# A hybrid attention and gated-recurrence layer: the recurrence's output gate as seven-product blocks, its queries computed ahead, its VectorE steps and root rewritten

## The chip, the cores and the metric

The kernel runs on one core of one Trainium2 chip. A core has a matrix engine (TensorE, PE in the profile, with PEld for its weight loads), three elementwise engines (VectorE or DVE, ScalarE or ACT, GpSimd or POOL) and SyncE (SP), which here issues DMA transfers. Each engine takes its own instructions in their order, and semaphores make one wait for another. The metric is the device time of one execution in microseconds.

## The reference

One layer on x (1024 tokens by 1024 channels, float32). After an RMS norm a single projection gives everything: queries, keys and values of 24 attention heads, a gate path for attention, and for the recurrence q, two forget gates, an input i and an output gate g, and two merge gates.

```python
z = einsum('bsd,dc->bsc', h, w_in)
qkv_a, g_a, q_b, zf_fwd, zf_bwd, i_b, g_b, zgate_a, zgate_b = split(z, split_points)
...
f = lb + (1.0 - lb) * sigmoid(z_f)                  # per direction
o = gla_chunk_scan(q_b, 1.0 - f, i_b, log(f))       # S_t = diag(f_t) S_{t-1} + k_t v_t^T, o_t = S_t^T q_t
...
o_b = rms_norm(o_fwd + o_bwd, hg_norm_w) * silu(g_b)
merged = sigmoid(zgate_a) * y_a + sigmoid(zgate_b) * y_b
out = x + merged @ w_out
```

Attention normalises its queries and keys per head (`rms_norm` again), in three groups of dilated windows. The recurrence has 8 heads of 128 channels and runs forwards and backwards.

## The kernel before, in words

**Arithmetic.** Big products are made in three passes: a float32 operand is split into a rounded high part and the rest (`whi` and `wlo` for weights, `hh` and `hl` for activations), and high by high, high by low and low by high are added up in PSUM. Each pass is a matmul of 128x128 weights by 512 columns. A weight page (128x512) comes by DMA, ACT rounds it (`whi<-raw` or `whi<-qraw`), and POOL, DVE or an adding DMA makes the rest (`wlo`).

**What sets the order.** The builder writes the program with a planner at its side. Each call is booked on a clock per engine (`note`, line 139), work that isn't a big product is queued as tasks with a priority and a condition, and after every few matmuls `tick` (line 253) and `burst` (line 269) put those into the program that the clocks call ready. The result is one fixed order of instructions on each engine. On the chip an engine that is late against these clocks delays all that stands behind it.

**The stages, in order.**

1. Values of the three attention groups as plain products (`gp` in the rows).
2. Blocks of seven products (`run_quads`, line 433): a pair of 512-channel halves by a pair of 512-token halves in 7 products of 12 matmuls in place of 8, as in Strassen's scheme. The products 11, T2, T3 and T4 go one after another into one PSUM bank (`qA`), T1 and 22 into a second (`qE`), 21 into a third (`qC`). After 11, T1 and T2 ACT copies the bank out (`spare<-qA`, `stage<-qA`, `spare<-qE`) before the next product adds to it; T4 is copied at the block's end. There are 20 blocks in the order twelve times `qk` (queries and keys) and eight others: groups of `qk qk sg`, six times, then `ga ga`. A `qk` result goes through the norm of its heads: ACT squares it and rounds the square (`ny<-spare`, `nhi<-ny`), PE sums over a head (`nss`), and `guess` (line 1072) makes the inverse root on ACT with Ln, Exp and Square; `newton` on DVE corrects it. `sg` (merge gates) is only stored. `ga` (attention's gate) goes through Sigmoid on ACT (`ga_sig`, line 1120). Before the stage one table of ACT's functions that has Ln and Exp is set (`blocks_start`, line 1011).
3. Attention and its merge, with the projections for the recurrence's input i and gate g between them (`evac_early`, line 1514): for each of four pairs of heads 8 groups of 24 matmuls, whose 512 columns are 256 of i and 256 of g, stored to `igD`.
4. The recurrence, head by head. Six groups of 24 matmuls a head: four for the two forget gates by two halves (`evac_f`, with Sigmoid in the copy) and two for q (`evac_q`). Between them, as small matmuls and tasks: `logs` (ACT), `sums` (DVE: k, scan `Bc`, differences), `exps_b` (ACT), `k_mul` (POOL), `q_mul` and `k_state` (DVE), transposes `kT`, states `U` and `S`, cross products `X` and `Y`, outputs `oB`, `norm_out` (DVE: root and product with the gate), transpose `onT`. The gate's Sigmoid is `gate_sig` on ACT. Merge gates (eight groups of 24) end the stage.
5. The last projections as seven products again (`sA`, `sE`), and the residual.

A tile's first letters name it in the profile; all work is booked through one helper, so all rows bear line 56 (57 in the changed kernel).

Of the kernel before, what the change touches and what calls it, by code (L numbers as in the profile page):

```python
# [27 lines left out]
TAIL, LATE = 4, 4  # L28
QRAW, SPARE = 6, 7
# [84 lines left out]
class Plan:  # L114
# [5 lines left out]
    def __init__(self, nc):  # L120
        self.nc = nc
        self.t = dict(pe=0.0, act=0.0, dve=0.0, pool=0.0, sp=0.0)
        self.port = 0.0
        self.wire = 0.0
        self.w, self.r = Book(), Book()
        self.wide = True
# [12 lines left out]
    def note(self, key, op, args, kw):  # L139
        if op == "preload_act_table_set":  # L140
            self.t["act"] += 1.3
            return
# [14 lines left out]
        for x in outs:  # L157
            start = max(start, self.w.last(x, key, self.HOP), self.r.last(x, key, self.HOP))
        if op == "dma_start":
# [6 lines left out]
        else:  # L166
# [45 lines left out]
class Builder:  # L212
# [128 lines left out]
    def feed(self):  # L341

        if self.raw_next < len(self.wpages):
            t = self.rawr.get()
            self.p.sp.dma_start(t, self.wpages[self.raw_next])
# [227 lines left out]
def hybrid_block(ctx, tc, a, out):  # L573
# [41 lines left out]
    ig_pages = lambda pr: some(100 + 20 * pr, 8)  # L615
# [5 lines left out]
    for k in range(6):  # L621
        blocks += qk[2 * k:2 * k + 2] + sg[k:k + 1]
    blocks += [("ga", 0), ("ga", 2)]

    def block_pages(kind, *at):
        if kind == "sg":
            return (*gate_pages(*at), *gate_pages(at[0], at[1] + 1))
        if kind == "ga":
            return tuple(some(72 + 2 * at[0], 4))
        g, hv, e = at  # L630
# [6 lines left out]
    for pr in range(4):  # L637
        items += ig_pages(pr)
    for j in range(TAIL, LATE):
        items += gate_pages(1, j)  # L640
    for h in range(8):
        items += zf_pages(h) + q_pages(h)
# [152 lines left out]
    igD = dr.tile([4, 8, 128, 512], F32, name="igD")  # L795
# [315 lines left out]
    def put_ga(j):  # L1111
        def f(half, col, z, mine):
# [4 lines left out]
            b.task("act", [z], lambda: ga_sig(j + col, half, z, ring), 3, blk["y"].soon)  # L1117
        return f

    def ga_sig(j, half, z, ring):  # L1120
# [8 lines left out]
        def out():  # L1129
            s_.dma_start(gaD[j, half], z)  # L1130
# [8 lines left out]
    b.run_quads(A, [{"qk": put_qk, "sg": put_sg, "ga": put_ga}[x[0]](*x[1:]) for x in blocks],  # L1139
# [374 lines left out]
    def evac_early(pr, i):  # L1514
        def f(ps):
# [3 lines left out]
            store(igD[pr, i], t)  # L1519
        return f  # L1520

    for pr in range(4):
# [8 lines left out]
        pos += 8  # L1531
    merge_maybe(True)
# [22 lines left out]
    nomlb = hp.tile([128, 2, 8], F32, name="nomlb")  # L1555
    a_.activation(lb, mx, AF.Sigmoid)
    v_.tensor_scalar(omlb, lb, -1.0, 1.0, op0=OP.mult, op1=OP.add)
    v_.tensor_scalar(nomlb, omlb, -1.0, None, op0=OP.mult)
# [13 lines left out]
    ig_ring = b.ring(hp, "ig", 8, [128, 512])  # L1572
    sk_ring = b.ring(hp, "sk", 5, [128, 512])
    qq_ring = b.ring(hp, "q", 3, [128, 512])
    lf_ring = b.ring(hp, "lf", 4, [128, 512])
    q2_ring = b.ring(hp, "q2", 4, [128, 4, 64])
    km_ring = b.ring(hp, "km", 4, [128, 512])
    qr_ring = b.ring(hp, "qr", 4, [128, 512])
# [7 lines left out]
    GI = set()  # L1586
    SK, QQ = {}, {}
    H = {}

    def load_ig(pr, i):  # L1590
        t = ig_ring.get()
        s_.dma_start(t, igD[pr, i])
        IG[pr, i] = t

    def gate_sig(pr, i):

        t = on_ring.get()
        for k in range(2):
            a_.activation(t[:, 256 * k:256 * k + 256], IG[pr, i + k][:, 256:512], AF.Sigmoid)
        b.task("dve", [t], lambda: gate_mul(pr, i, t), 5)  # L1600

    def gate_mul(pr, i, t):
        for k in range(2):
            g = IG[pr, i + k][:, 256:512]
            v_.tensor_tensor(g, g, t[:, 256 * k:256 * k + 256], op=OP.mult)
        on_ring.done(t)
        GI.add((pr, i))
# [25 lines left out]
    def start_head(h):  # L1633
        st = dict(mm=[None, None], G=[None, None], QR={}, Q2={}, KM={}, S={}, s=0, qm=0, km=0)
# [3 lines left out]
        b.task("act", [SK[h, d, u] for d, u in ORDER], lambda: logs(h), 4, lambda: lf_ring.soon(4))  # L1638

    def logs(h):  # L1640
        a_.preload_act_table_set("natural_log_exp_and_others")
        for d, u in ORDER:
            lf = lf_ring.get()
# [3 lines left out]
    def sums(h, d, u, lf):  # L1647
        st = H[h]
        sk = SK[h, d, u]
        v_.tensor_scalar(sk, sk, nomlb[:, d, h:h + 1], omlb[:, d, h:h + 1], op0=OP.mult, op1=OP.add)  # L1650
# [6 lines left out]
        for k, e in enumerate((MID1[d], MID2[d], LAST[d])):  # L1657
            g_.tensor_copy(st["mm"][d][:, k, 4 * u:4 * u + 4], B4[:, :, e])
# [7 lines left out]
        b.task("act", [D1, Q2], lambda: exps_b(h, d, u, D1, Q2), 4, lambda: km_ring.soon() and qr_ring.soon())  # L1666

    def exps_b(h, d, u, D1, Q2):
# [3 lines left out]
        a_.activation(c4(KM)[:, :, fst], c4(D1)[:, :, fst], AF.Exp, scale=-1.0)  # L1672
        a_.activation(c4(KM)[:, :, sec], Q2, AF.Exp, scale=-1.0)
        QR = qr_ring.get()
        a_.activation(QR, D1, AF.Exp)
        a_.activation(Q2, Q2, AF.Exp)
        lf_ring.done(D1)
        st["QR"][d, u], st["KM"][d, u] = QR, KM
        b.task("pool", [KM], lambda: k_mul(h, d, u), 3)
        if h % 2 == 0 and len(st["QR"]) == 4:  # L1680
            for i in range(0, 8, 2):
                b.task("act", [], lambda i=i: gate_sig(h // 2, i), 4, lambda i=i: (h // 2, i + 1) in IG and on_ring.soon())
# [4 lines left out]
    def decay(h, d):  # L1687
# [5 lines left out]
        v_.tensor_tensor(t[:, cur], mm[:, 2, cur], mm[:, 0, nxt], op=OP.add)  # L1693
        v_.tensor_tensor(G[:, cur, d], t[:, cur], mm[:, 0, cur], op=OP.subtract)
        v_.tensor_tensor(G[:, cur, 1 - d], t[:, cur], mm[:, 1, cur], op=OP.subtract)
# [38 lines left out]

    def k_state(h, d, u):
# [4 lines left out]
        ks = SK.pop((h, d, u))  # L1740
# [582 lines left out]
```

## Time and profile before

| what | value |
|---|---|
| median of 3 runs (lowest, highest) | 1514.19 us (1513.56, 1517.37) |
| the profiled execution, its span | 1514.28 us, 1512.5 us |
| instructions | 23147, of which 8013 matmuls |
| busy: PE, DVE, ACT, POOL | 1472.8, 1004.8, 873.7, 411.2 us |
| stage 2, seven-product blocks | from 148.2 us to about 563 |
| stage 4, recurrence | from about 869 us to 1305 |

The span runs from the first to the last instruction. In the profile's rows an engine's busy time comes with its count of instructions; a mean is that of one instruction; what stands behind the bar is the time that the engine idled just before instructions of that group, and whom it waited for. One fp32 matmul that isn't split (128x128 by 128) shows as two.

### The profile page before, as it was taken

Reading aid. Unit: us, or ns where it says so; the run is one execution under the profiler, and the core shown is the slowest. Engines: PE = TensorE matmul, PEld = TensorE weight load, DVE = VectorE, ACT = ScalarE, POOL = GpSimd, SP = SyncE. Lnnn points to the kernel's source line nnn. Section 1 sums busy time; section 2 is a strip of 40 time slices with the busy share of each in tenths; the row PEclk is TensorE's granted clock in tenths of the full one; section 3 lists DMA queues with packets and bytes.
Section 4 is the critical chain, followed back from the end, with each engine's and each line's share of the span. In section 5 each row is a group of like instructions: output and inputs, shape, how many; then the busy total and the mean of one; then the engine's idle time right before and its main releaser. Section 6 shows DMA issues by size and latency. Waiting matters only on the chain.

```text
span 1512.5 us, 23147 instructions
## 1 busy us (share of the span) xinstructions
PE 1472.8 (97%) x8013; PEld 1211.2 (80%) x8013; DVE 1004.8 (66%) x2061; ACT 873.7 (58%) x1788; POOL 411.2 (27%) x436
## 2 busy tenths in 40 slices
PE   8999999999999999999999998999999999999998
PEld 6788878778788887888877787888878888887787
DVE  6791677678878854545423636988688887259873
ACT  5542667476676755676742266575567664447451
POOL 0032334344443340020023342333244322000011
PEclk9999999999999999999999999999999999999999
DMA  6454465755744347566265673353434524775554
GB/s 201 134 201 161 155 200 120 193 110 135 175 112 119 99 131 262 173 215 190 84 169 181 190 207 68 70 140 78 132 65 90 135 65 101 209 237 167 168 154 132
DMA packets 181067, 224.08 MB, mean 148 GB/s; under 512 B 45084, under 2 KB 101428, under 8 KB 180437
## 3 DMA queue, kind: packets, MB, share of 16 engines
q1 hardware_dynamic: 158980, 195.67, 40.5%
q0 software_dynamic: 14544, 26.48, 11.3%
q10 hardware_dynamic: 7424, 0.45, 0.3%
q8 instruction: 63, 1.03, 0.3%
q14 instruction: 56, 0.45, 0.1%
HBM read 166.61 MB, written 77.43 MB: 161 GB/s over the span
## 4 chain that ended last, share of the span: by engine, by line
PE 59%; ACT 3%; issue 3%; DVE 3%; DMA 2%; POOL 1%; SPq 0%; POOLq 0%; ACTq 0%; DVEq 0%
PE gp L56 25%; PE sA L56 6%; PE qA L56 5%; PE sE L56 4%; PE qE L56 3%; PE o L56 3%; PE oB L56 3%; PE pT L56 2%; PE sc L56 2%; PE U L56 1%; PE qC L56 1%; PE X L56 1%; ACT L56 1%; DMA raw<-in_w_in_dram 1%; DVE Bc L56 1%
## 5 line engine op out<-in xcount | busy, mean ns | idle before, releaser
L56 POOL TENSOR_TENSOR wlo<-qraw,whi 128x512 fp32r<-128x512 f32 x100 | 148.2, 1487 | 259.4 <-ACT whi L56 230.5
L56 PE MATMUL gp<-whi,hh 128*128 128x512 f32 x344 | 139.2, 405 | 3.2 <-ACT stage L56 1.8
L56 PE MATMUL gp<-hh,whi 128*128 128x512 f32 x336 | 137.6, 409 | 0.0
L56 PE MATMUL gp<-whi,hl 128*128 128x512 f32 x344 | 134.8, 392 | 1.4 <-DVE hl L56 1.3
L56 PE MATMUL gp<-wlo,hh 128*128 128x512 f32 x344 | 134.5, 391 | 1.4 <-POOL wlo L56 1.4
L56 PE MATMUL gp<-hh,wlo 128*128 128x512 f32 x336 | 131.9, 392 | 0.0
L56 PE MATMUL gp<-hl,whi 128*128 128x512 f32 x336 | 131.4, 391 | 0.0
L56 ACT ACTIVATE whi<-qraw 128x512 fp32r<-128x512 f32 x140 | 86.9, 626 | 72.2 <-DVE qraw L56 48.6
L56 POOL TENSOR_TENSOR wlo<-raw,whi 128x512 fp32r<-128x512 f32 x46 | 64.6, 1417 | 234.9 <-ACT whi L56 232.4
L56 ACT ACTIVATE whi<-raw 128x512 fp32r<-128x512 f32 x120 | 74.9, 626 | 85.5 <-PE gp L56 66.1
L56 DVE CUSTOM_DVE_ANT_0 as<-sc,abias 128x192 f32<-128x192 f32 (+2 forms) x192 | 56.0, 348 | 91.8 <-PE sc L56 71.4
L56 ACT ACTIVATE stage<-gp 128x512 f32<-128x512 f32 x60 | 35.6, 598 | 108.2 <-PE gp L56 71.9
L56 DVE TENSOR_TENSOR qraw<-qraw,qraw 128x512 f32<-128x512 f32 x80 | 66.5, 832 | 42.7 <-DMA qraw<-in_w_in_dram 21.5
L56 POOL DMA_DIRECT2D wlo<-in_w_in_dram x49 | 43.4, 885 | 162.3 <-ACT wlo L56 144.0
L56 ACT ACTIVATE as<-as,neg 128x192 f32<-128x192 f32 (+2 forms) x192 | 83.5, 439 | 6.1 <-DVE neg L56 6.1
L56 PEld LDWEIGHTS gp<-whi,hh 128*128 128x128 f32 x344 | 64.6, 188 | 23.3 <-issue 4.8
L56 PEld LDWEIGHTS gp<-whi,hl 128*128 128x128 f32 x344 | 64.6, 188 | 16.6 <-DVE hl L56 3.0
L56 PEld LDWEIGHTS gp<-wlo,hh 128*128 128x128 f32 x344 | 64.7, 188 | 14.7 <-POOL wlo L56 2.7
L56 PEld LDWEIGHTS gp<-hh,wlo 128*128 128x128 f32 x336 | 63.3, 189 | 14.0
L56 PEld LDWEIGHTS gp<-hl,whi 128*128 128x128 f32 x336 | 63.7, 190 | 11.2
L56 PEld LDWEIGHTS gp<-hh,whi 128*128 128x128 f32 x336 | 63.6, 189 | 11.0
L56 ACT ACTIVATE ny<-ny 128x512 f32<-128x512 f32 x96 | 60.7, 633 | 11.4 <-DVE ny L56 5.5
(295 smaller groups left out, 4179.0 us busy)
## 6 DMA issues: line engine op xcount, KB each, us to landing
raw<-in_w_in_dram SPq DMA_DIRECT2D x112, 256.0 KB
qraw<-in_w_in_dram SPq DMA_DIRECT2D x80, 256.0 KB
wlo<-in_w_in_dram POOLq DMA_DIRECT2D x49, 256.0 KB, 3.9
qkD<-ny SPq DMA_DIRECT2D x48, 256.0 KB
igD<-stage SPq DMA_DIRECT2D x32, 256.0 KB
ig<-igD SPq DMA_DIRECT2D x32, 256.0 KB
sg<-sgD SPq DMA_DIRECT2D x32, 256.0 KB
eraw<-wsD SPq DMA_DIRECT2D x32, 256.0 KB
```

The costliest lines, as they stand in the source:

```text
L56: got = f(*args, **kw)
```

## The change

It has six parts.

- **The output gate g.** It leaves the plain products of stage 3. Four new blocks `gb` of seven products stand in stage 2, one behind each of the first four groups (`qk qk sg gb`); their results go through `ga_sig` (Sigmoid on ACT, product on DVE, in place) to `gbD`, one row per channel. Stage 3 has then two sets of 8 groups for i alone (`ibD`).
- **The queries q.** Their 16 groups move from stage 4 to stage 3, behind those of i, and are stored to `qD`; stage 4 loads them again, and loads the gate.
- **VectorE's steps.** k is no longer made by a DVE instruction of its own: `exps_b` adds log(1-lb) to its exponents on ACT, and `k_mul` makes (sigmoid - 1) times that on DVE, where it stood on POOL before; the minus sign is undone by the corrected root (its factor -0.5 is left out with 1/256 in `onw`). The forget gate's copy is a plain copy now, and its Sigmoid a second ACT instruction in `logs`, four in a row.
- **The root.** `norm_out`'s eleven small DVE instructions become Ln, Exp, Square on ACT and two on DVE, then four scaled copies on ACT; the gate is multiplied in behind the transpose, by one DVE instruction that also empties the bank.
- **The rings.** i takes 8 tiles of half the width, the gate 2, loaded q 2, forget gates 7 for 5; the logs, their differences and exponentials share 8 tiles.
- **The planner** books a change of ACT's function table (`self.table`), and DVE's wait for its own results.

On ACT in stage 2, inside a pair of `qk` blocks: two guesses (Ln, Exp, Square: the first reads `nss`) between two copies of a bank. Before:

```order
L56 ACTIVATE spare_2235<-qA_2103 128x512
L56 ACTIVATE whi_2244<-qraw_1956 128x512
L56 ACTIVATE ny_2253<-nss_2210,eps 128x512
L56 ACTIVATE ny_2253<-ny_2253 128x512
L56 ACTIVATE ny_2254<-ny_2253 128x512
L56 ACTIVATE whi_2265<-qraw_2141 128x512
L56 ACTIVATE ny_2272<-nss_2237,eps 128x512
L56 ACTIVATE ny_2272<-ny_2272 128x512
L56 ACTIVATE ny_2273<-ny_2272 128x512
L56 ACTIVATE whi_2290<-qraw_2133 128x512
L56 ACTIVATE stage_2316<-qA_2297 128x512
```

And in the changed kernel, in the pair behind the first `gb` block:

```order
L57 ACT_TABLE_LOAD
L57 ACTIVATE ny_2503<-nss_2452,eps 128x512
L57 ACT_TABLE_LOAD
L57 ACTIVATE ny_2503<-ny_2503 128x512
L57 ACTIVATE ny_2504<-ny_2503 128x512
L57 ACTIVATE whi_2519<-qraw_2313 128x512
L57 ACT_TABLE_LOAD
L57 ACTIVATE ny_2527<-nss_2481,eps 128x512
L57 ACT_TABLE_LOAD
L57 ACTIVATE ny_2527<-ny_2527 128x512
L57 ACTIVATE ny_2528<-ny_2527 128x512
L57 ACTIVATE spare_2542<-qA_2272 128x512
```

A load of a function table stands ahead of each Ln and each Exp now. So it is with 40 of the 48 guesses; the eight ahead of the first `gb` block have none.

On ACT in stage 4, around the first head (`km`, `lf`, `qr`, `q` belong to the forget gates, `on` to the output gate, `kT` is a transposed key). Before:

```order
L56 ACT_TABLE_LOAD
L56 ACTIVATE on_8794<-ig_8471 128x256
L56 ACTIVATE on_8794<-ig_8473 128x256
L56 ACTIVATE on_8805<-ig_8475 128x256
L56 ACTIVATE on_8805<-ig_8477 128x256
L56 ACTIVATE whi_8816<-raw_8597 128x512
L56 ACTIVATE wlo_8817<-whi_8816 128x512
L56 ACT_TABLE_LOAD
L56 ACTIVATE G_8789<-G_8789 128x14
L56 ACTIVATE kT_8827<-kT_8822 128x512
L56 ACT_TABLE_LOAD
L56 ACTIVATE sk_8845<-gp_8797 128x512
```

After, for the second head:

```order
L57 ACTIVATE kT_9467<-kT_9462 128x512
L57 ACTIVATE kT_9473<-kT_9469 128x384
L57 ACTIVATE sk_9475<-gp_9403 128x512
L57 ACT_TABLE_LOAD
L57 ACTIVATE sk_9281<-sk_9281 128x512
L57 ACTIVATE sk_9341<-sk_9341 128x512
L57 ACTIVATE sk_9475<-sk_9475 128x512
L57 ACTIVATE sk_9401<-sk_9401 128x512
L57 ACT_TABLE_LOAD
L57 ACTIVATE qr_9493<-sk_9281,lbv,omlb 128x512
L57 ACTIVATE qr_9495<-sk_9341,lbv,omlb 128x512
L57 ACTIVATE kT_9535<-kT_9530 128x512
```

Here the loads are fewer, two a head, and stand together; no key's copy stands between them.

On DVE in stage 4, first head: k (`sk`), scan (`Bc`), differences, and in the changed kernel the key product `km`. Before:

```order
L56 TENSOR_SCALAR sk_8605<-sk_8605,nomlb,omlb 128x512
L56 SCALAR_TENSOR_TENSOR Bc_8697<-rst_8437,lf_8618 128x512
L56 TENSOR_TENSOR lf_8618<-Bc_8697 128x512
L56 TENSOR_TENSOR q_2_8703<-Bc_8697 128x256
L56 TENSOR_TENSOR Gt_8740<-mm_8607 128x7
L56 TENSOR_TENSOR G_8739<-Gt_8740,mm_8607 128x7 x2
```

After:

```order
L57 SCALAR_TENSOR_TENSOR Bc_9323<-rst_9074,qr_9249 128x512
L57 TENSOR_TENSOR qr_9249<-Bc_9323 128x512
L57 TENSOR_TENSOR q_2_9328<-Bc_9323 128x256
L57 SCALAR_TENSOR_TENSOR km_9330<-sk_9130,km_9330 128x512
L57 SCALAR_TENSOR_TENSOR km_9347<-sk_9164,km_9347 128x512
L57 TENSOR_TENSOR Gt_9371<-mm_9234 128x7
L57 TENSOR_TENSOR G_9370<-Gt_9371,mm_9234 128x7 x2
```

One row is gone, and POOL's product has come in. The diff, cut to what is spoken of:

```diff
@@ note (planner)
+        if key == "dve":
+            for x in ins:
+                start = max(start, self.w.last(x) + 0.05)
...
+                need = {AF.Sigmoid: ("sig",), AF.Ln: ("ln",), AF.Exp: ("exp", "ln")}.get(args[2])
+                if need and self.table not in need:
+                    self.table = need[0]
+                    pace += 1.28
@@ pages and blocks
-    ig_pages = lambda pr: some(100 + 20 * pr, 8)
+    ib_pages = lambda k: [_dram(wi, (100 + 40 * k + d) * 65536, [[512, 128], [20 * 65536, 2], [1, 256]]) for d in range(8)]
...
-        blocks += qk[2 * k:2 * k + 2] + sg[k:k + 1]
+        blocks += qk[2 * k:2 * k + 2] + sg[k:k + 1] + ([("gb", k)] if k < 4 else [])
@@ put_ga
+    def put_gb(pr):
+        return put_ga(2 * pr, gbD)
@@ stage 3
-    for pr in range(4):
+    for pr in range(2):
...
+    for h in range(EARLY):
+        for u in range(2):
+            b.run_unit([T_group(pos, u, evac_qe(h, u), u == 1)])
+            merge_maybe()
+        pos += 2
@@ stage 4
-            a_.activation(t, ps, AF.Sigmoid)
+            a_.activation(t, ps, AF.Copy)
...
     def logs(h):
+        for d, u in ORDER:
+            a_.activation(SK[h, d, u], SK[h, d, u], AF.Sigmoid)
         a_.preload_act_table_set("natural_log_exp_and_others")
...
-        v_.tensor_scalar(sk, sk, nomlb[:, d, h:h + 1], omlb[:, d, h:h + 1], op0=OP.mult, op1=OP.add)
...
-        a_.activation(c4(KM)[:, :, fst], c4(D1)[:, :, fst], AF.Exp, scale=-1.0)
+        a_.activation(c4(KM)[:, :, fst], c4(D1)[:, :, fst], AF.Exp, scale=-1.0, bias=lomlb[:, d, h:h + 1])
...
-        g_.tensor_tensor(KM, KM, SK[h, d, u], op=OP.mult)
+        v_.scalar_tensor_tensor(KM, SK[h, d, u], -1.0, KM, op0=OP.add, op1=OP.mult)
...
-        r = rsqrt(b, tiny, ss, 4, 1.0 / 128, "o")
-        for c in range(4):
-            f0 = 128 * c
-            v_.scalar_tensor_tensor(on[:, f0:f0 + 128], ps[:, f0:f0 + 128], r[:, c:c + 1],
-                                    IG[pr, 4 * u + c][:, 256 + 128 * sub:384 + 128 * sub], op0=OP.mult, op1=OP.mult)
+    def norm_guess(h, u, ps, on, ss):
+        y, y2 = (tiny.tile([128, 4], F32, tag=k, name=b.name(k), bufs=3) for k in ("oy", "oz"))
+        a_.activation(y, ss, AF.Ln, scale=1.0 / 128, bias=eps)
+        a_.activation(y, y, AF.Exp, scale=-0.5)
+        a_.activation(y2, y, AF.Square)
+        def newton():
+            v_.scalar_tensor_tensor(y2, ss, 128 * EPS, y2, op0=OP.add, op1=OP.mult)
+            v_.scalar_tensor_tensor(y, y2, -384.0, y, op0=OP.add, op1=OP.mult)
...
-        a_.activation(t, ps, AF.Copy, scale=hwc)
+        v_.scalar_tensor_tensor(t, ps, onw, GB[h, u], op0=OP.mult, op1=OP.mult)
```

More of the change, by code (lines that the diff above doesn't have):

```diff
@@ L28 @@
 TAIL, LATE = 4, 4
+EARLY = 8
 QRAW, SPARE = 6, 7
@@ L1591, in load_ig, with load_q_early, load_gb @@
         t = ig_ring.get()
-        s_.dma_start(t, igD[pr, i])
+        s_.dma_start(t, ibD[pr // 2, i, :, 256 * (pr % 2):256 * (pr % 2) + 256])
         IG[pr, i] = t
[L1595 to L1607, printed above, removed]
+    def load_q_early(h, u):
+        t = qq_ring.get()
+        s_.dma_start(t, qD[h, u])
+        QQ[h, u] = t
+    def load_gb(h, u):
+        t = gb_ring.get()
+        s_.dma_start(t, gbD[h, u])
+        GB[h, u] = t
+    SK, QQ = {}, {}
     def evac_f(h, d, u):
@@ L1812, in cross @@
         b.product(6, [xa], lambda: outputs(h, u, xa),
-                  lambda: st["s"] == 4 and on_ring.soon() and (h // 2, 4 * u + 2) in GI
+                  lambda: st["s"] == 4 and on_ring.soon() and all((h // 2, 4 * u + c) in IG for c in range(4))
                   and b.when_all(list(st["S"].values())), merge=False)
```

139 lines of the change are left out of this document (87 added, 52 removed).

## The prediction, made before the changed kernel had been run

> **What bounds the kernel now.** I read the page's head, then the engines' busy time by stage, then PE's waits, and last single instructions.
>
> ```profile
> span 1512.5 us, 23147 instructions
> PE 1472.8 (97%) x8013; PEld 1211.2 (80%) x8013; DVE 1004.8 (66%) x2061; ACT 873.7 (58%) x1788; POOL 411.2 (27%) x436
> ...
> core 0: us, PE busy (x) PEld busy (x) DVE busy (x) ACT busy (x) POOL busy (x), PEclk, DMA share, GB/s
> 148.20:568.90 420.70, 412.38 (x1801) 338.16 (x1799) 313.24 (x375) 275.30 (x473) 178.16 (x136) 1.00 0.55 142
> 893.00:1262.00 369.00, 355.89 (x2234) 302.45 (x2233) 297.37 (x689) 238.01 (x438) 133.19 (x191) 0.99 0.40 95
> ...
> PE U L56 <- ACT kT L56: 7.6, 3, 3.6
> PE oB L56 <- DVE S L56: 5.2, 3, 1.9
> PE nss L56 <- ACT nhi L56: 4.1, 1, 4.1
> ```
>
> PE is the bound in every stage; its waits add up to some 30 us, so the time is the sum of its matmuls plus those waits. Second in line are ACT and DVE: in the block stage ACT is busy 275.3 of 420.7 us (473 instructions, 0.58 us each) and DVE 313.2; in the recurrence ACT 238.0 and DVE 297.4 of 369.
>
> What one wide matmul takes is the distance of starts, since busy spans overlap:
>
> ```profile
> 869.23 0.39 PE L56 MATMUL gp<-hh,whi 128*128 128x512 f32 x1
> ...
> 879.88 0.39 PE L56 MATMUL gp<-hh,wlo 128*128 128x512 f32 x1
> ```
>
> These are 47 starts apart: 10.65 / 47 = 0.2266 us. I sum against the profiled execution, 1514.28 us; the median of the runs is 0.1 us below.
>
> **Matmuls.** i and g took 4 x 8 x 24 = 768 matmuls. Now i takes 2 x 8 x 24 = 384 and g four blocks of 7 x 12 = 336: 48 fewer, **-10.9 us**. By stages: the block stage gets 336 more (+76.1), the recurrence loses q's 16 x 24 = 384 (-87.0), and attention's stage has 384 of i and 384 of q where it had 768, so nothing there: a cover of the same length for attention's small products, with as many page splits, copies and stores.
>
> **The price in the block stage.** What the order shows is 84 more loads of ACT's function table there (two in each of 40 guesses, one for each new gate block). The stage had one:
>
> ```profile
> L56 ACT ACT_TABLE_LOAD x1 | 1.3, 1283 | 0.0
> ...
> 1013.53 0.63 ACT L56 ACTIVATE wlo<-whi 128x512 fp32r<-128x512 f32 x1
> 1014.18 1.28 ACT L56 ACT_TABLE_LOAD   x1
> 1015.47 0.42 ACT L56 ACTIVATE km<-lf 128x256 f32<-128x256 f32 x1
> ...
> 412.82 0.58 ACT L56 ACTIVATE spare<-qA 128x512 f32<-128x512 f32 x1
> 413.45 0.50 PE L56 MATMUL qA<-S2h,whi 128*128 128x512 f32 x1 [0.65 <-ACT spare L56]
> ```
>
> The first row is the stage's, the next three are from the recurrence: a load holds ACT 1.28 us, and the instruction behind it starts at once. So 84 x 1.283 = 108 us of ACT. The last two rows are the gate through which ACT reaches PE: PE waits with the next product into a bank until ACT has copied it, and between the product and that next one lies a single other product, 12 x 0.2266 = 2.7 us. ACT can't fall behind by more than that without stopping PE.
>
> The Trainium skill (page ScalarE: Activation LUTs, section What ACT_TABLE_LOAD costs) gives 1283 ns for the load, and 1380 ns more for a drain at each switch. The load's length agrees with the rows above, the drain doesn't show there; with it the 84 switches would hold ACT for 223 us, an estimate by that page.
>
> Does it fit? Over the whole stage yes: ACT has 420.7 - 275.3 = 145 us of idle time, and the gate blocks bring 76 us of PE for 4 x 15 x 0.58 = 35 us of ACT. In the pairs of `qk` blocks it doesn't. One such block has 31 ACT instructions (7 splits, 4 copies, 4 x 5 for the norm): 18.0 us, to 92 x 0.2266 = 20.8 us of PE. With 8 loads it has 28.3. Ten blocks stand behind the first gate block: 10 x 7.4 = 74 us, the upper end. A part flows into the `sg` and `gb` blocks behind, which are light on ACT. The order gives the lower end: from the copy `stage_2474` to the copy `stage_2789` ACT has 43 instructions and 12 loads, 43 x 0.58 + 12 x 1.283 = 40.3 us, and PE has 154 matmuls between the ends of these, 34.9 us. That is 5.4 us in each of five pairs, 27 us. Two shorter pile-ups stand ahead of it in a pair, two guesses before a copy each; I give them 2.5 us together, so 8 a pair, 40 us. That is nearer to the lower end, because it counts what is on ACT between two gates rather than in a block. A long stop also costs clock:
>
> ```profile
> 303.98 0.50 PE L56 MATMUL nss<-nhi,headones 128*128 128x512 f32 x1 [4.07 <-ACT nhi L56]
> ...
> 304.00:306.00 2.00, 1.78 (x4) 1.27 (x5) 0.79 (x2) 1.94 (x4) 0.00 (x0) 0.66 0.00 0
> 306.00:308.00 2.00, 2.00 (x6) 1.51 (x6) 1.97 (x3) 1.97 (x5) 1.09 (x1) 0.50 0.00 0
> ```
>
> Behind a stop of 4.07 us there are 10 matmuls in 4 us where 17.6 fit: 1.7 us lost. Four or five stops of that size: 7 us. Together **+47 us**, between 27 and 82. ACT late also makes DVE late (`newton` waits for a guess), which I don't price; it lies in the upper end.
>
> The gate blocks' other work: 16 sums of raw pages, 12 sums of banks, 8 low parts and 16 products on DVE, by the rows below at most 16 x 0.825 + 20 x 0.72 + 16 x 1.2 = 47 us in 76 us of new PE time, less than the stage's share of 74%; POOL's 20 more splits lie in its idle 58%. Nothing.
>
> ```profile
> L56 DVE TENSOR_TENSOR qraw<-qraw,qraw 128x512 f32<-128x512 f32 x76 | 62.7, 825 | 26.6 <-DMA qraw<-in_w_in_dram 21.5 <-POOL wlo L56 5.1
> L56 DVE TENSOR_TENSOR wlo<-qraw,whi 128x512 fp32r<-128x512 f32 x39 | 28.1, 720 | 37.8 <-ACT whi L56 37.8
> L56 DVE TENSOR_TENSOR stage<-stage,ny 128x512 f32<-128x512 f32 x6 | 7.1, 1201 | 5.7 <-ACT ny L56 5.7
> ```
>
> **The recurrence** gets PE's 369 - 87 = 282 us for the same small work.
>
> ```profile
> L56 DVE TENSOR_SCALAR sk<-sk,nomlb,omlb 128x512 f32<-128x512 f32 x32 | 29.1, 908 | 32.9 <-ACT lf L56 32.9
> L56 DVE SCALAR_TENSOR_TENSOR on<-oB,rr,ig 128x128 f32<-128x128 f32 x56 | 15.8, 345 | 1.6
> L56 DVE TENSOR_TENSOR ig<-ig,on 128x256 f32<-128x256 f32 x32 | 11.4, 419 | 0.1
> L56 DVE SCALAR_TENSOR_TENSOR rt<-rt,rv 128x4 f32<-128x4 f32 x42 | 7.9, 188 | 1.4
> L56 DVE SCALAR_TENSOR_TENSOR ny<-nss,ny 128x512 f32<-128x512 f32 x48 | 32.8, 684 | 15.3 <-ACT ny L56 15.3
> L56 POOL TENSOR_TENSOR km<-km,sk 128x512 f32<-128x512 f32 x32 | 47.2, 1513 | 10.6 <-ACT km L56 10.6
> L56 ACT ACT_TABLE_LOAD x33 | 42.3, 1283 | 1.4 <-PE gp L56 0.8
> ...
> 907.35 1.28 ACT L56 ACT_TABLE_LOAD   x1
> 909.26 1.28 ACT L56 ACT_TABLE_LOAD   x1
> 912.11 1.28 ACT L56 ACT_TABLE_LOAD   x1
> 915.94 1.28 ACT L56 ACT_TABLE_LOAD   x1
> 917.36 0.58 ACT L56 ACTIVATE kT<-kT 128x512 f32<-128x512 f32 x1
> ```
>
> DVE loses 29.1 for k, 64 x 0.345 = 22 and 11.4 for the gate, and 16 x 11 small ones at about 0.18 (32): 95 us. It gets 48 wide ones at 0.684 (32 in `k_mul`, 16 behind the transpose) and 32 small ones: 39 us. So 297 - 56 = 241 of 282 us, 85% where it was 81%; POOL's 47 us in `km` go, and with them what slowed DVE beside it. ACT gets 32 Sigmoids at 0.58, 64 scaled copies of 128x128 (between 0.2 and 0.41, its rows of 14 and 256 columns; I take 0.28) and 48 tiny ones, 47 us; it loses 17 loads (22), 32 splits for q at 0.63 (20), and 32 gate Sigmoids, 16 copies of q and 16 of the output (32). That makes some 211 of 282, 75% for 65%. Loads and stores of q and g add 48 SP issues, which wait for nothing that PE needs within a head.
>
> PE's six stops there are 7.6 + 5.2 = 12.8 us. The longer ones stand behind four table loads ahead of a key's copy (last five rows above); the changed order has none between the keys' copies but in a block of eight ahead of a head. Against that, both engines are fuller. I take **-4 us**, between -16 (no stop, and none of the 3 to 4 us that a clock of 0.99 costs in 369) and +35 (below).
>
> **Sum.** 1514.3 - 10.9 + 47 - 4 = **1546 us**.
>
> **The rivals.**
>
> *The loads are hidden* (other side). If the copies reach PE in time, because the guesses run while ACT would have idled, only the matmuls count: 1514.3 - 10.9 - 4 = 1499 us. For it: ACT's 145 us idle. Against it: those 40.3 us between two gates for 34.9 of PE, with no wait of ACT in the sum at all. It decides from where a pair's run takes less than its 34.9 us. 7%; that half is hidden and about +11 us eats the matmuls (1512 to 1519): 5%.
>
> *One load a guess.* If Ln's load also served Exp, 44 of the 84 would stay: the run is 40.3 - 6 x 1.283 = 32.6 us, below PE's 34.9, and the loss at most 10 x (23.1 - 20.8) = 23 us; with a third of that, 1507 us. The order has a load ahead of each Exp: 2%. The Trainium skill (ScalarE: Activation LUTs, section Table sets: the hidden batching unit) states that Ln and Exp share one set and need one load; this program's order shows two per guess, so its rule doesn't rule here.
>
> *DVE becomes the bound of the recurrence.* It idles 369 - 297 = 72 us there in waits for ACT and PE. If these stay while PE's cover shrinks, a stretch lasts 241 + 72 = 313 us, not 282: +31, and +4 for the gain not made: 1581 us. 9%.
>
> *A pause as long as the load behind each switch*, 84 x 1.28 us more on ACT: 15.4 us more in a run, five times: 1546 + 77 = 1623 us. The row at 1015.47 speaks against it: 2%. This is what the drain in the Trainium skill (ScalarE: Activation LUTs, section What ACT_TABLE_LOAD costs) would do.
>
> **Chances and range.** The forecast has 75%; the loads hidden have 7, half hidden 5, one load a guess 2, DVE 9, the pause 2. Its own bounds are 1514.3 - 10.9 + 27 - 16 = 1514 and 1514.3 - 10.9 + 82 + 0 = 1585; a gain of all of 16 and the least loss together are unlikely, so 1520 to 1585 holds eight in ten. About 0.3% (4.5 us) is what a measurement can tell from no change. Faster: 7 + 2 = 9%; the same: 5%; slower: 86%.
>
> **What would show it.** Right: the block stage about 120 us longer with 85 loads, ACT over 80% busy there, PE's waits headed by `qA` behind `spare` and `stage`, several over 4 us and a granted clock under 1 behind them; the recurrence shorter by about 90 us, with `U` no longer waiting 3 us for `kT`. Wrong: waits of PE in the block stage under 20 us in all, a recurrence shortened by less than 70, or loads followed by a pause.

## The result, and the profile after

The changed kernel takes 1584.72 us (median of 4 runs, 1584.02 to 1585.43) against 1515.78 us (4 runs, 1513.56 to 1520.14) for the kernel before, timed on the same chip. The ratio is 1.0451, with an interval from 1.0425 to 1.0477. It is slower by some 69 us, where 32 had been forecast.

The page's head of the changed kernel, with the loads of ACT's tables among its groups:

```profile
span 1583.2 us, 23063 instructions
...
PE 1489.0 (94%) x7965; PEld 1216.0 (77%) x7965; DVE 975.7 (62%) x1890; ACT 994.3 (63%) x1963; POOL 365.6 (23%) x376
...
L57 ACT ACT_TABLE_LOAD x107 | 137.3, 1283 | 8.6 <-PE gp L57 5.5
```

The 48 matmuls are gone (7965 for 8013), ACT's loads have gone from 39 to 107, and PE's share has fallen from 97 to 94%. Now the engines' busy time in four stretches: blocks of seven products, attention and merge, recurrence with its merge gates up to the merge's first product on DVE (`ma<-gp,sg`), and the rest.

```profile
core 0: us, PE busy (x) PEld busy (x) DVE busy (x) ACT busy (x) POOL busy (x), PEclk, DMA share, GB/s
149.40:730.20 580.80, 507.94 (x2116) 408.74 (x2115) 360.86 (x426) 418.05 (x615) 198.37 (x156) 0.95 0.42 115
730.20:1044.50 314.30, 311.88 (x2185) 251.31 (x2184) 139.26 (x544) 168.77 (x536) 59.44 (x62) 1.00 0.59 188
1044.50:1370.30 325.80, 323.98 (x2197) 279.24 (x2196) 239.45 (x521) 241.09 (x512) 73.77 (x119) 1.00 0.48 125
1370.30:1583.20 212.90, 201.30 (x848) 161.06 (x846) 138.87 (x220) 95.83 (x167) 10.36 (x12) 0.97 0.53 165
```

Cut at the same places, the two traces compare like this:

| stretch | before | after | difference | its matmuls | what is left |
|---|---|---|---|---|---|
| up to the blocks | 148.0 | 149.4 | +1.4 | 0 | +1.4 |
| blocks | 415.5 | 580.7 | +165.2 | +76.1 | +89.1 |
| attention and merge | 313.3 | 314.4 | +1.1 | 0 | +1.1 |
| recurrence | 433.6 | 325.8 | -107.8 | -87.0 | -20.8 |
| last stage | 202.1 | 212.9 | +10.8 | 0 | +10.8 |

The sum is 70.7 us, as between the two spans. So nearly the whole loss arises in the blocks (the last stage adds 10.8 us), and the recurrence gave more than forecast. PE's waits in the changed kernel:

```profile
PE qA L57 <- ACT stage L57: 23.1, 6, 6.2
PE nss L57 <- ACT whi L57: 18.6, 3, 9.3
PE nss L57 <- DVE ny L57: 14.6, 5, 5.4
PE qA L57 <- ACT spare L57: 10.1, 5, 2.5
PE sA L57 <- ACT xh L57: 6.4, 2, 5.4
PE nss L57 <- DVE nlo L57: 3.4, 2, 1.9
...
PE qA L57 <- DVE spare L57: 2.0, 2, 1.5
...
PE qA L57 <- DVE stage L57: 1.2, 1, 1.2
```

All the `qA` and `nss` rows lie in the blocks: 36.4 us at the copies of a bank (before: 2.7) and 36.6 us at the sums over a head (before: 5.6). Stops of PE add up to 73.0 us there, 65 more than before. Of the other 24 us some 19 stand behind the stops, where the granted clock is low (0.95 over the stretch, 1.00 before): the clock is at half behind the ten longest of the 24 stops, those of 2.58 to 9.34 us, and by the trace's clock records PE works some 41 us at half clock (3 before); the rest isn't taken apart. The shortest of these ten stops, with the busy time around it:

```profile
588.78 0.51 PE L57 MATMUL qA<-S2h,whi 128*128 128x512 f32 x1 [2.58 <-ACT stage L57]
588.00:593.00 5.00, 4.22 (x12) 3.31 (x13) 3.41 (x3) 2.92 (x6) 3.54 (x2) 0.66 0.08 31
```

The longest stop, 9.34 us, in the timelines of ACT, DVE and PE:

```profile
643.46 1.28 ACT L57 ACT_TABLE_LOAD   x1
644.76 0.69 ACT L57 ACTIVATE ny<-nss,eps 128x512 f32<-128x512 f32 x1
645.47 1.28 ACT L57 ACT_TABLE_LOAD   x1
646.76 1.29 ACT L57 ACTIVATE ny<-ny 128x512 f32<-128x512 f32 x2
647.96 0.61 ACT L57 ACTIVATE whi<-qraw 128x512 fp32r<-128x512 f32 x1
648.59 1.28 ACT L57 ACT_TABLE_LOAD   x1
649.88 0.69 ACT L57 ACTIVATE ny<-nss,eps 128x512 f32<-128x512 f32 x1
650.59 1.28 ACT L57 ACT_TABLE_LOAD   x1
651.88 1.29 ACT L57 ACTIVATE ny<-ny 128x512 f32<-128x512 f32 x2
653.08 0.58 ACT L57 ACTIVATE stage<-qA 128x512 f32<-128x512 f32 x1
653.55 0.62 ACT L57 ACTIVATE whi<-qraw 128x512 fp32r<-128x512 f32 x1
...
654.21 0.69 DVE L57 TENSOR_TENSOR wlo<-qraw,whi 128x512 fp32r<-128x512 f32 x1 [8.84 <-ACT whi L57]
654.81 0.69 DVE L57 TENSOR_TENSOR qraw<-qraw,qraw 128x512 f32<-128x512 f32 x1
655.42 0.68 DVE L57 SCALAR_TENSOR_TENSOR ny<-nss,ny 128x512 f32<-128x512 f32 x1
...
656.25 0.77 PE L57 MATMUL nss<-nhi,headones 128*128 128x512 f32 x1 [9.34 <-ACT whi L57]
```

Read it backwards. PE stands at the next sum over a head, whose bank is free only when `newton` on DVE has read the one before (`ny<-nss,ny`, 655.42 to 656.10; the view names ACT's `whi`, but that had ended at 654.17, 2 us before PE went on). That instruction stands on DVE behind a weight's low part, and this waits 8.84 us for the weight's high part, which ACT makes at 653.55, behind two guesses with four loads. No load is followed by a pause: the next instruction starts 1.29 to 1.30 us after the load's start.

ACT isn't full. In one group of four blocks (two `qk`, then `sg`, then `gb`), cut at the first product of each, most of PE's idle time comes in the third block, though the norms that ACT works off there belong to the second:

```profile
332.60:352.60 20.00, 20.00 (x90) 16.52 (x88) 11.60 (x16) 12.48 (x20) 10.49 (x10) 1.00 0.79 180
352.60:375.10 22.50, 20.36 (x89) 16.45 (x88) 15.68 (x19) 18.04 (x28) 11.42 (x11) 1.00 0.62 118
375.10:409.20 34.10, 24.07 (x94) 18.95 (x92) 15.96 (x22) 26.23 (x36) 10.30 (x10) 0.89 0.49 118
409.20:435.20 26.00, 22.25 (x86) 17.77 (x85) 17.08 (x18) 16.97 (x23) 7.12 (x5) 0.88 0.30 92
```

These four take 102.6 us, with some 20 us of matmuls each. ACT is busy 62, 80, 77 and 65% in them, and yet PE stops.

In the recurrence, cut out of the trace alone, the stops behind the key's copy are gone, and of the 12.8 us in six stops before 0.8 us are left:

```profile
PE oB L57 <- DVE S L57: 0.8, 2, 0.4
PE gp L57 <- issue: 0.7, 1, 0.7
PE Y L57 <- ACT kT L57: 0.3, 1, 0.3
```

The last stage has a new one, here in PE's timeline:

```profile
1441.58 0.79 PE L57 MATMUL sA<-xh,whi 128*128 128x512 f32 x1 [5.42 <-ACT xh L57]
```

And the engines' busy time in the four microseconds behind it, where 10 matmuls ran and 17.6 fit:

```profile
1442.00:1446.00 4.00, 4.00 (x10) 2.92 (x10) 2.99 (x6) 1.63 (x3) 0.00 (x0) 0.50 0.17 61
```

### The profile page after: what moved, and what is told of

Same layout as the page of the kernel before. It is cut to its first block, busy times and chain, and to the rows that moved or that the text cites. A ratio compares the mean times of both kernels' runs of the same rounds, so it can differ in the third digit from the quotient of the medians.

```text
span 1583.2 us, 23063 instructions
## 1 busy us (share of the span) xinstructions
PE 1489.0 (94%) x7965; PEld 1216.0 (77%) x7965; DVE 975.7 (62%) x1890; ACT 994.3 (63%) x1963; POOL 365.6 (23%) x376
## 4 chain that ended last, share of the span: by engine, by line
PE 58%; ACT 9%; issue 4%; DVE 4%; DMA 1%; SPq 0%; POOL 0%; ACTq 0%; DVEq 0%; POOLq 0%
PE gp L57 26%; PE qA L57 7%; PE sA L57 5%; PE sE L57 3%; ACT L57 3%; PE o L57 3%; ACT ny L57 3%; PE oB L57 2%; PE qE L57 2%; PE sc L57 2%; PE pT L57 2%; ACT whi L57 1%; PE U L57 1%; PE qC L57 1%; PE X L57 1%
## 5 line engine op out<-in xcount | busy, mean ns | idle before, releaser
L57 POOL TENSOR_TENSOR wlo<-qraw,whi 128x512 fp32r<-128x512 f32 x120 | 170.5, 1427 | 403.2 <-ACT whi L57 376.8
L57 ACT ACTIVATE whi<-qraw 128x512 fp32r<-128x512 f32 x168 | 103.1, 624 | 66.0 <-DVE qraw L57 36.2
L57 PE MATMUL gp<-whi,hh 128*128 128x512 f32 x248 | 100.9, 407 | 2.1 <-ACT hh L57 1.5
L57 PE MATMUL gp<-whi,hl 128*128 128x512 f32 x248 | 97.3, 392 | 1.4 <-DVE hl L57 1.3
L57 PE MATMUL gp<-wlo,hh 128*128 128x512 f32 x248 | 96.8, 390 | 0.0
L57 DVE TENSOR_TENSOR wlo<-qraw,whi 128x512 fp32r<-128x512 f32 x48 | 33.4, 696 | 79.3 <-ACT whi L57 79.2
L57 PE MATMUL qA<-hh,whi 128*128 128x512 f32 x192 | 77.3, 403 | 3.1 <-DVE spare L57 2.0
L57 DVE SCALAR_TENSOR_TENSOR ny<-ny,spare 128x512 f32<-128x512 f32 x48 | 76.1, 1585 | 1.6
L57 PE MATMUL qA<-hh,wlo 128*128 128x512 f32 x192 | 76.5, 398 | 0.0
L57 PE MATMUL qA<-hl,whi 128*128 128x512 f32 x192 | 76.5, 398 | 0.0
```

The source lines that it names most:

```text
L57: got = f(*args, **kw)
```

## The experiments

The theory: the loads of ACT's tables make the blocks' loss. The rivals: the gate blocks' other work makes it, or the order that the planner wrote does. Where no number of runs stands with a time, it is from one run. The kernels are the changed one with the edit shown, unless the text names another as the start. "Loss" is a block stage's time over its matmuls at 0.2266 us each: 2112 of them (478.6 us), and 1776 (402.6 us) in the kernel before, whose loss is 12.9 us; the changed kernel's is 102.1.

**One table set for the root.** Ahead of a guess that follows a Sigmoid, the set that holds both Ln and Exp is set by hand. The order of instructions is otherwise the changed kernel's, but for a few rows on ACT and DVE.

```diff
     def guess(g, hv, e, half, col, z, ps):
+        if b.p.table == "sig":
+            a_.preload_act_table_set("natural_log_exp_and_others")
         a_.activation(y, ps, AF.Ln, scale=1.0 / 64, bias=eps)
```

> The changed kernel with ACT's table of Ln and Exp set again ahead of the first guess behind a Sigmoid, nothing else: 31 table loads in the program for 107, and nearly the same order of everything else. Theory (the loads make the loss in the block stage, 90 us of 166 beyond its own 76 us of matmuls): the block stage comes to 490 to 505 us, the whole to 1495 to 1510. Rival (the gate blocks themselves, their DVE sums or the planner's new rules make the loss): over 1550.

1507.32 us (4 runs), against 1518.22 for the kernel before: 0.9929, from 0.9904 to 0.9954. The stage has 9 loads and takes 503.0 us, a loss of 24.4; attention takes 315.3, the recurrence 326.4, the last stage 212.1. Two lines turn a loss of 4.5% into a gain of 0.7%.

**The loads alone.** The kernel before, with one 128x1 Sigmoid, which nobody uses, behind the first `sg` block:

```diff
     def put_sg(w, j):
         def f(half, col, z, mine):
+            if (w, j, half, col) == (0, 0, 0, 0):
+                a_.activation(flip[:, 0:1], eps, AF.Sigmoid)
```

> The kernel before with one Sigmoid of 128x1 on ACT behind the first sg block, into a spare tile: 128 table loads for 39, no gate block, the same order of all other instructions. Theory (loads alone make the loss): about 1590 to 1620, since 44 guesses with two loads each come in a stage that has no gate blocks to take up the lag. Rival (loads hide and the gate blocks cost): under 1540.

1599.44 us. 128 loads for 39; the stage takes 497.2 us, a loss of 94.6. Nothing else of the change is in it: 89 more loads cost 82 us in this stage. One tiny instruction is enough, since after it the program never finds the set with both functions again and loads twice in each guess.

**One load in each guess.** The set is set by hand ahead of every Ln, and the planner books that load:

```diff
     def guess(g, hv, e, half, col, z, ps):
+        a_.preload_act_table_set("natural_log_exp_and_others")
         a_.activation(y, ps, AF.Ln, scale=1.0 / 64, bias=eps)
```

> The changed kernel with one table load ahead of every guess (Ln and Exp in one set): about 44 fewer loads than the changed kernel. If only what ACT has beyond PE's work between two bank copies counts, the loss nearly goes: 32.6 us of ACT against 34.9 of PE in a run, 1500 to 1520 in all. If each load costs PE its own length in proportion, half of the loss stays: 1540 to 1550.

1525.36 us, between the two ranges, nearer the first: the stage has 53 loads, takes 519.1 us and loses 40.5. But its order differs, since the planner knew of every load.

**Both loads booked.** The planner books Ln, Exp and Sigmoid as three tables, as the program has them:

```diff
-                need = {AF.Sigmoid: ("sig",), AF.Ln: ("ln",), AF.Exp: ("exp", "ln")}.get(args[2])
-                if need and self.table not in need:
-                    self.table = need[0]
+                need = {AF.Sigmoid: "s", AF.Ln: "l", AF.Exp: "e"}.get(args[2])
+                if need and need not in self.table:
+                    self.table = need
                     pace += 1.28
```

> The changed kernel with a planner that books both loads of a guess; 109 loads, so the same work of ACT and another order around it. Theory (the amount of ACT's work between the copies sets the loss): 1560 to 1590. Rival (the order is wrong because the planner did not know of the second load, and a stop comes from work standing too early): under 1545.

1538.4 us: the rival's side. The stage has 87 loads, as many as the changed kernel to within two, and loses 53.9 us where that loses 102.1. So about half of the loss, 48 us, belongs to the order: the changed kernel's planner takes Ln's load to serve Exp and the next guesses too, and so books a load only at a Sigmoid and at the return from one, 9 in the stage, where the chip makes 85.

**The planner's booking of DVE taken out.** As the first experiment, and without the new rule that DVE waits for its own results:

```diff
-        if key == "dve":
-            for x in ins:
-                start = max(start, self.w.last(x) + 0.05)
```

> As e1 (one table set ahead of each guess's Ln behind a Sigmoid), but the planner no longer books DVE's wait for its own results (0.05 us behind each operand); the arithmetic is e1's, the order on the engines isn't. In e1 the last stage, from the merge's first product on, takes 212.1 us for 202.1 before the change, with a stop of PE of 5.4 us (sA behind xh) and a halved clock behind it. Theory: DVE booked as slower makes the planner put merge's work ahead of the sum that the last projections wait for; without the rule the stop is gone, the last stage is back at 202 to 204 us and the kernel takes 1495 to 1501 us. Rival: the stop comes from how the recurrence's end is laid out now (fewer products there as cover, whatever the planner books): last stage 211 to 214 us, 1504 to 1511 us.

1499.03 us (2 runs), 0.9879 of the kernel before (0.9831 to 0.9927), as the theory had it, but not by its sum. The stop in the last stage is gone and that stage takes 206.0 us. The blocks lose only 9.3 us (487.9), a gain of 15 that I hadn't thought of, attention takes 311.3; the recurrence and the last stage together take 550.9 for 538.5. (The place where the merge begins moves with the order, so these two are compared as a sum.) The rule harms the blocks and helps the recurrence.

**The Sigmoid back in the copy.** As the first experiment, with the forget gate's Sigmoid in its copy out of the bank:

```diff
     def evac_f(h, d, u):
-            a_.activation(t, ps, AF.Copy)
+            a_.activation(t, ps, AF.Sigmoid)
...
     def logs(h):
-        for d, u in ORDER:
-            a_.activation(SK[h, d, u], SK[h, d, u], AF.Sigmoid)
```

> As e1, but the forget gate's Sigmoid goes back into its copy out of the bank, so that it isn't four in a row in logs: 78 table loads in all for e1's 31. In the recurrence (from the first copy of a forget gate to the merge's first product) e1 takes 326.4 us, where 433.6 before less 87 for q's products would be 346.6. Theory: fewer loads of tables are what took PE's stops away; with the Sigmoid in the copy the stops behind kT and gp come back, the recurrence takes 340 to 350 us and the kernel 1521 to 1531. Rival: the DVE and POOL steps did it (k's instruction and POOL's product gone): the recurrence stays within 326 to 331 us and the kernel at 1505 to 1512.

1531.68 us. The recurrence takes 352.3 us with 63 loads for 17, and with the last stage 560.5 for 538.5. The stops behind the key's copy are back, in the view of PE's waits within the recurrence:

```profile
PE U L57 <- ACT kT L57: 13.0, 9, 2.1
PE oB L57 <- DVE S L57: 3.9, 5, 1.5
PE kT L57 <- DVE sk L57: 2.6, 2, 1.7
```

ACT is busy 285 of 352 us, which isn't full either.

**The key in two steps again.** As the first experiment, but DVE subtracts 1, and POOL multiplies:

```diff
     def exps_b(h, d, u):
+        sk = SK[h, d, u]
+        v_.tensor_scalar(sk, sk, 1.0, -1.0, op0=OP.mult, op1=OP.add)
...
-        b.task("dve", [KM], lambda: k_mul(h, d, u), 3)
+        b.task("pool", [KM], lambda: k_mul(h, d, u), 3)
...
-        v_.scalar_tensor_tensor(KM, SK[h, d, u], -1.0, KM, op0=OP.add, op1=OP.mult)
+        g_.tensor_tensor(KM, KM, SK[h, d, u], op=OP.mult)
```

> As e1, but the key is made in two steps again: DVE subtracts 1 from the Sigmoid (32 instructions of some 0.9 us), and POOL multiplies (32 of some 1.5 us) where DVE does it in one now. Theory (loads of tables made the recurrence's gain): the recurrence stays within 326 to 331 us, the kernel at 1505 to 1512. Rival (the DVE and POOL steps made it): recurrence 335 to 350 us, kernel 1516 to 1531.

1516.74 us. The recurrence takes 339.2 us, and with the last stage 545.7 for 538.5: a loss of 7 us, against 22 us with the loads back. Each of these two kernels also has an order of its own, and without the rule on DVE a new order alone cost the same two stretches 12 us. So the loads stand behind the greater part, with their stops behind the key's copy as the sign; that the 7 us belong to the steps on DVE and POOL isn't shown.

**The queries left in the recurrence.** As the first experiment, with none made ahead:

```diff
-EARLY = 8
+EARLY = 0
```

> As e1, but the queries' 16 groups (384 products, 87 us) stay in the recurrence instead of being made ahead during attention and merge. My prediction took the move as neutral there: attention's small products had a cover of 768 products before and have one of 768 after. If PE was full in both places, attention's stretch is 315 - 87 = 228 us and the recurrence 326 + 87 = 413, the kernel within 1503 to 1511. Rival (attention's stretch needs the cover that q gives it): attention's stretch 240 to 270 us, the recurrence 413, the kernel 1520 to 1550. A second rival (the recurrence needs more cover than it has after the change): the recurrence under 408, the kernel under 1502.

1563.7 us: the first rival, and more. The engines' busy time in attention's stretch and in the recurrence:

```profile
650.10:935.20 285.10, 240.30 (x1815) 188.33 (x1814) 134.29 (x544) 150.49 (x504) 38.16 (x46) 0.89 0.57 178
935.20:1354.20 419.00, 411.89 (x2571) 349.37 (x2570) 241.19 (x521) 269.59 (x561) 88.05 (x135) 1.00 0.47 108
```

And PE's longest waits in attention's stretch alone:

```profile
PE al L57 <- DVE og L57: 17.4, 11, 2.7
PE alT L57 <- DVE mx L57: 14.6, 3, 14.2
```

Without the queries attention's stretch takes 285.1 us, not 228: its small products run out of cover, and PE stops for 45 us at a clock of 0.89. The recurrence and last stage take 626.3 us, 538.5 and the 87 of the products. So, once the gate has left attention, the move of the queries is worth 57 us.

**No load in the blocks, same order.** The changed kernel, its order kept on every engine, the gate tiles' Sigmoid made an Exp (so the kernel's output is another):

```diff
     def ga_sig(dst, z, ring):
-        a_.activation(t, z, AF.Sigmoid)
+        b.p.gate = True
+        a_.activation(t, z, AF.Exp)
+        b.p.gate = False
```

> The changed kernel with its order kept row for row on all engines, but with Exp for the Sigmoid of the 48 gate tiles of the block stage (the gates' values are then others; the planner is still told of a Sigmoid), so that no load of a table stands in that stage: 21 loads for 107. Theory (the loads make the whole loss, the gate blocks' other work none): the stage takes its matmuls' 478.6 us and the 13 us that it lost before the change, 488 to 496 us for 580.7; the kernel 1490 to 1500. Rival (the gate blocks' DVE and POOL work, or their PSUM banks, cost too): the stage takes 503 us or more, the kernel over 1505.

1506.78 us. The stage takes 501.2 us, a loss of 22.6: between the theory and the rival. The loads make 79.5 of the changed kernel's 102.1 us. 9.7 stay over the kernel before. The two runs without the rule on DVE in this stage (losses of 9.3 above and 10.6 below, both under the 12.9 of before) have the gate blocks too, so these 9.7 go with the planner's booking and not with the gate blocks' own work.

**One load a guess, same order.** As the third, but the planner isn't told, so the order is the changed kernel's row for row:

```diff
     def guess(g, hv, e, half, col, z, ps):
+        a_.real.preload_act_table_set("natural_log_exp_and_others")
         a_.activation(y, ps, AF.Ln, scale=1.0 / 64, bias=eps)
```

> The changed kernel with its order kept row for row, but one table load in each guess for two, set by hand ahead of every Ln and not told to the planner (75 loads for 107). The stage's loss over its matmuls is 102 us with two loads a guess and 24 with one at each return from a Sigmoid only (9 in the stage). Theory (ACT falls behind only where a run between two copies outgrows PE's work, so the second load does most of the harm): loss 25 to 45 us, stage 504 to 524, kernel 1507 to 1527. Rival (each load costs the same): about 24 + 78 x 44/76 = 69 us, stage 548, kernel 1551.

1545.66 us, the rival's side: the stage, with 53 loads, takes 539.2 us and loses 60.6. The stops are at the same two places as with two loads, by PE's waits and by the busy time of the stage:

```profile
PE qA L57 <- ACT stage L57: 16.7, 7, 3.7
PE nss L57 <- ACT whi L57: 10.9, 3, 6.8
PE nss L57 <- DVE ny L57: 8.7, 2, 4.8
```

```profile
148.80:688.00 539.20, 498.84 (x2115) 403.37 (x2114) 361.22 (x426) 378.36 (x583) 197.35 (x156) 0.97 0.46 124
```

With one order (but for the few rows of the first experiment, which gives the second point) there are now four points:

| loads in the stage | loss, us | price of one more load |
|---|---|---|
| 0 | 22.6 | |
| 9 | 24.4 | 0.2 |
| 53 | 60.6 | 0.8 |
| 85 | 102.1 | 1.3 |

The price is an average over the loads added. It rises to a load's whole length, 1.28 us, though ACT idles 28% of the stage in the changed kernel.

**The booking of DVE in the recurrence only**, with one table set for the root:

```diff
-        if key == "dve":
+        if key == "dve" and self.rule:
...
+    b.p.rule = True
     bctx = ExitStack()
     hp = bctx.enter_context(tc.tile_pool(name="hgrn", bufs=1))
...
+    b.p.rule = False
     for j in range(LATE, 8):
```

> One table set a guess behind a Sigmoid (as in e1), and the planner's booking of DVE's wait for its own results only from the start of the recurrence to the merge gates. Without that booking anywhere (e5) the block stage took 487.9 us for e1's 503.0, attention 311.3 for 315.3, but recurrence and last stage together 550.9 for 538.5. If the booking's worth goes by stage: 488 + 311 + 538, the kernel at 1484 to 1490 us. If the recurrence's gain hangs on what stood before it in the order: 1494 to 1502.

1488.06 us (5 runs, 1483.9 to 1490.25) against 1518.68 (9 runs) for the kernel before: 0.9791, from 0.9769 to 0.9813. It beats both kernels, and the stages do add up but for attention's (315.2, not 311), as the engines' busy time in the same four stretches shows:

```profile
148.80:638.00 489.20, 484.15 (x2115) 397.58 (x2114) 353.58 (x426) 320.75 (x538) 200.25 (x156) 1.00 0.52 137
638.00:953.20 315.20, 311.32 (x2176) 251.32 (x2176) 138.10 (x544) 168.83 (x537) 59.12 (x62) 0.99 0.60 188
953.20:1282.40 329.20, 327.10 (x2209) 281.76 (x2209) 239.66 (x520) 240.95 (x512) 73.79 (x119) 1.00 0.48 124
1282.40:1488.50 206.10, 197.69 (x845) 157.82 (x843) 138.39 (x220) 95.07 (x167) 10.35 (x12) 1.00 0.57 170
```

**The booking kept to the end**, as the last but without the line that takes it back:

```diff
-    b.p.rule = False
     for j in range(LATE, 8):
```

> As e10, but the booking stays on to the end of the kernel. If it is what puts the stop of 5.4 us (sA behind xh) into the last stage, that stop is here and not in e10, and this kernel takes 5 to 9 us more than e10. If not, the two agree within 2 us.

1491.71 us (2 runs). The stop is back, in PE's timeline:

```profile
1350.58 0.80 PE L57 MATMUL sA<-xh,whi 128*128 128x512 f32 x1 [5.90 <-ACT xh L57]
```

The last stage takes 212.2 us for 206.1, as expected. The whole kernel loses only 3.7, less than the 5 to 9 forecast, and one of its runs (1489.46) lies within the range of the other kernel's five; in the profiled execution what stands ahead of the last stage came out 2.8 us shorter. Most of that is attention, 312.1 us for 315.2 in the same order: a few us in a stretch of one execution, as in the attention of the run without the rule, show nothing. The rule alone doesn't make the stop: with the Sigmoid in the copy, or the key in two steps, it is on in the last stage too and that takes 208.2 and 206.5 us. It goes with the one order that came out.

## Why the prediction was wrong in its size

The direction was right, and ACT's loads, the mechanism named, make most of the loss. The time lies 0.3 us inside the upper end of the range, and that is luck: the blocks' loss lies above the 82 us that I had as its upper end, the recurrence's gain beyond the -16 that I had as its best, and the two errors partly cancel. The sum missed by 39 us, and its terms one by one:

| term | predicted | measured |
|---|---|---|
| 48 matmuls | -10.9 | -10.9 |
| blocks, beside matmuls | +47 | +89.1 |
| attention | 0 | +1.1 |
| recurrence, beside matmuls | -4 | -20.8 |
| last stage and start | 0 | +12.2 |
| sum | +32 | +70.7 |

**The step that failed** is the size of the block stage's term: "8 a pair, 40 us", taken nearer to the lower end "because it counts what is on ACT between two gates rather than in a block". The count of loads (84 more), their length, and the lack of a pause behind them were right. The copies of a bank, the one gate that was priced, cost about what I said: 36.4 us of stops, 33.7 more than before, for 40. But there is a second gate, the sums over a head, with 31 us more of stops: PE waits for DVE's `newton` to free their bank. I named that lateness and left it in the upper end. The third part is the clock, some 19 us where I took 7: I had counted four or five long stops, and behind ten the clock was halved.

The upper end, 10 blocks by 7.4 us and with the clock 82, is close to the 79.5 us of the loads in this order. I had left it because part of the work flows into the `sg` and `gb` blocks, which have little on ACT. It does flow there, but there PE stops for it (10 of the 34.1 us in the third block above), since PE, DVE and ACT each keep their order and wait for one another in a ring, as in the longest stop. That the two numbers are so close may still be chance.

What I put at nothing without a reason is the order itself as a cause. About half of the loss goes when the planner books both loads (53.9 for 102.1), and 10 us (15 in the kernel with the table set by hand) came from its new booking of DVE, which stands in the diff and which I passed over. With an order that fits two loads, the loss over the kernel before is 53.9 - 12.9 = 41 us. That this is near to my 47 is chance, since the booking of DVE is in it too.

**The recurrence** was better than its -4, and by the table better than the end of its range (-16), which stood for no stop and no lost clock; together with the last stage it gained 10. The loads' batching took the stops behind the key's copy: with the loads back the two stretches lose 22 us. The key in two steps costs them 7, which may be its order. The two sum to more than the 10 gained, and no run takes out the rest of the change there. DVE as the bound there was the rival with 9%: it is busy 239 of 326 us, 73%, so that rival fell. Part of the gain was given back in the last stage, by a stop of 5.4 us and a halved clock, which no term of mine held; some 4 us of that stage's 10.8 stay unexplained, since without the stop it still takes 206 us for 202.

**The signs** that I had set: the block stage is 165 us longer, not 120; ACT is busy 418 us of it, the sum as forecast, but 72% and not over 80, because the stage had grown; PE's waits are headed by `qA` behind `stage`, with stops of up to 6.2 us there, and of up to 9.3 and 5.4 us at the sums over a head, which I hadn't named; the recurrence is shorter by 108 us for 90 and `U` waits no more.

**The rivals.** The loads weren't hidden, and no pause stands behind them. One load a guess, which I gave 2%, isn't what the program does by itself; made by hand it takes 1525 us in an order that knows of it and 1546 in the changed kernel's, not the 1507 that I had worked out for it, since the loads that stay cost more than I thought. 1507 us come out where loads stand only at a Sigmoid and at the return from one. The Trainium skill (ScalarE: Activation LUTs, section Table sets: the hidden batching unit) says that Ln and Exp need one load, as one set holds both. The first experiment agrees once that set is named: 9 loads in the stage for 85. Left to itself the program loads twice.

## What to carry to other kernels

Where engines wait for one another in a ring, a load on an engine with idle time can be paid at its full length when there are many: price it by the chain from the engine to every gate of the bound one (copies, sums, banks freed by a third engine), not by the gate that is easiest to count. Before a function of another set goes between functions that share one, set the shared set by hand after it, and see in the order how many loads each use has. When an order is written from booked costs, a cost that the chip has and the planner hasn't spoils the order on top of the cost itself: here about as much again (102.1 us for 53.9).

## What the runs showed of the hardware

- A single 128x1 Sigmoid put 89 more loads into the kernel and cost 81 us of 1518, in one run: what stands ahead of a pair of Ln and Exp in the program decides whether it gets two loads or none.
- The price of a load rose with their number, from 0.2 to 1.3 us each, in one fixed order, while the engine that loads was busy 72% of the stage at the most loads, and at most about 80% in the blocks of the group shown.
- Behind a stop of 5.42 us PE's matmuls started 0.43 us apart for some 4 us, at a granted clock of 0.50. The Trainium skill (TensorE: Matmul & The Clock Gate, section Part 1: The HAM clock gate) has the clock halved once PE was idle for a window of about 3.4 us, until it was busy for as long. The trace agrees for this stop, and not quite for shorter ones: in the block stage a stop of 2.58 us had a halved clock behind it too (0.66 over the 5 us shown), while the next shorter, 2.48 and 2.46 us, had none (1.00 over the 5 us from 637.0 and the 6 us from 614.0). In that stage the halved clock made some 19 us more on 65 us more of stops.
- Taking 384 products out of attention's stretch freed only 30 of their 87 us there.
